# Splitting the mixer's weights during the down projection before it

## The chip, the cores and the metric

The kernel runs on one core of a Trainium2 chip. The metric is the device time of one execution in microseconds; lower is better. The engines are PE (TensorE, matrix products), DVE (VectorE), ACT (ScalarE), POOL (GpSimd) and SP (SyncE, which here only issues DMAs). Each works through its own instructions in order.

## The reference

A first block (attention and a mixture of experts, not touched here) is followed by a second block of two layers on x, 512 tokens of 1024 features, all in float32. Each layer is a gated feed-forward, a mixer and another gated feed-forward, with a layernorm behind each:

```python
def _swiglu(x, wg, wu, wd):
    return (jax.nn.silu(x @ wg) * (x @ wu)) @ wd

def _mixer(x, w_in, ...):
    u = x @ w_in                                        # 1024 -> 1792
    u_conv, u_lru, q, k, v = jnp.split(u, [o1, o2, o3, o4], axis=-1)
    y_conv = _conv_module(u_conv, ...)                  # 31 taps, layernorm, silu
    y_lru = _recurrent(u_lru, ...)                      # 4 taps, gates, linear scan
    y_attn = _swa(q, k, v, band_bias, valid, sinks)     # 8 heads, a band of 128 keys
    return jnp.concatenate([y_conv, y_lru, y_attn], axis=-1) @ w_out

def second_block(x, ...):
    for l in range(DEPTH_2):                            # 2 layers
        h = 0.5 * _swiglu(x, ffn_w_gate[l, 0], ffn_w_up[l, 0], ffn_w_down[l, 0])
        x = _layernorm_2(ALPHA * x + h, ln_g[l, 0], ln_b[l, 0])
        h = _mixer(x, w_in[l], ...)
        x = _layernorm_2(ALPHA * x + h, ln_g[l, 1], ln_b[l, 1])
        h = 0.5 * _swiglu(x, ffn_w_gate[l, 1], ffn_w_up[l, 1], ffn_w_down[l, 1])
        x = _layernorm_2(ALPHA * x + h, ln_g[l, 2], ln_b[l, 2])
    return x
```

## The kernel before

Activations lie feature-major, [128 features, 8 blocks, 512 tokens]. Every float32 product is made of three faster ones (`mm3`, lines 191 to 197): weights and operands are split into a high part (a rounded copy, `wh`, `xh`) and the rest (`wl`, `xl`), and PE adds low times high, high times low and high times high. Activations are split where they are made. Weights are split on the way from DRAM, each time they are used: `chunk` (lines 153 to 167) loads 2048 columns, 1 MB, through SP's queue into one of two buffers `raw`, and `split` (lines 185 to 187) casts each piece of up to 1024 columns on ACT to `wh` and subtracts on DVE to `wl`. The pool `spl` has four buffers for `wh` and four for `wl`, so that a piece can be split when PE has done with the piece four before it. The loads and the splits of a chunk are given a priority ahead of the work around them (`AHEAD`); a scheduler turns priorities and dependences into one fixed order for each engine.

`second` (lines 1447 to 1454) runs six phases: feed-forward 0, mixer 0, feed-forward 1, feed-forward 2, mixer 1, feed-forward 3. A feed-forward (`ffn`, lines 1124 to 1151) makes 22 gated tiles `hh`, `hl` and then the down projection, a loop over d = 0 to 7: 66 products into `y` with pieces of 1024, 1024 and 768 columns of `w_d`, and for each d the layernorm's sums (`Norm.sums`: `x<-x,y` on DVE, line 1047, a square `q` on ACT, line 1054). The last d goes by halves of the tokens, so that `Norm.finish` (statistics, then the norm's outputs `xh`, `xl`) can work on the first half while PE does the second. `Norm.finish` also starts the next phase's first two weight chunks (`first_chunks`). The next phase begins with `first_tiles` (products `ft`), by halves too. The operand lies in the pool `xs`, four buffers [128, 2048]: two for `xh`, two for `xl`; they are in use until the last gate or up product, and again when the next norm writes its outputs.

The mixer (lines 1184 to 1444): the first four tiles; `project(j)` (lines 1228 to 1235) for the chunks 2, 6, 4 and, between the attention steps, 5 and 3 of `w_in2`, two output tiles `t` each; then eight attention steps. `scores` makes the scores in PSUM, DVE adds the bias and takes the maximum (line 1304), ACT the exponential `p` (line 227), DVE scales; `values` transposes `p` on PE (`pT`), copies it on ACT to `pt` (line 1338) and multiplies with the values on PE (`po`, line 1342). The scores of two steps are ahead of the values. On DVE the 62 taps of the convolution (`acc`, line 1220) fill the time from the first tiles on. The out projection takes the four chunks of `w_out2`: 0 from the seventh attention step on, 1 and 2 behind the attention (2 in buffers of its own, `qh` and `ql`), 3 at the end, with the mixer's layernorm by halves.

POOL does two memsets and two small loads (`bt`, the bias, and `wg`) at the start of a mixer, and nothing in a feed-forward.

Of the kernel before, what the change touches and what calls it, by code (L numbers as in the profile page):

```python
# [7 lines left out]
F32 = mybir.dt.float32  # L8
F32R = mybir.dt.float32r
# [5 lines left out]
P = 128  # L15
# [13 lines left out]
PIECE = 1024  # L29
# [33 lines left out]
class Pieces:  # L63
    """2048 columns of weights in DRAM, taken 512 at a time in small buffers"""
# [10 lines left out]
class Core:  # L75
    """The engines, the pools and the pieces that every phase uses."""
# [34 lines left out]
    @contextmanager  # L111
    def banks(self, **tags):
        """the 8 banks of PSUM for a phase: how many for a tag; a name that is no tag counts as any"""
        with self.tc.tile_pool(name="psum", bufs=1, space=bass.MemoryType.PSUM, reuse_waits="tile") as pool:
            old, self.psum = self.psum, (pool, tags)
            yield
            self.psum = old
# [27 lines left out]
    def more_raws(self, *sources, own_first=False):  # L145
        """buffers for loads before the two of every phase: (pool, tag, how many)"""
        self.raws, self.turn, self.pair = [], -1, None
        for pool, tag, n in sources + ((self.rawp, "raw", 2),):
            self.raws = self.raws + [(pool, tag)] * n
        if own_first:  # L150
            self.turn -= 2

    def chunk(self, src, n=2048, room=None):
        """n columns of weights in two parts each: pieces of up to 1024 columns"""
        with self.tc.high_priority(offset=self.ahead):
            r = self.load(src, n) if src.space == bass.MemoryType.DRAM else src
            w = Weights()
            for o in range(0, n, PIECE):
                m = min(PIECE, n - o)
                if room is None:  # L160
                    h = self.spl.tile([P, PIECE], F32R, name="wh", tag="wh")
                    l = self.spl.tile([P, PIECE], F32R, name="wl", tag="wl")
                else:
                    h, l = room(o)
                self.split(h[:, :m], l[:, :m], r[:, o:o + m])
                w.append((h, l))
        return w

    def first_chunks(self, src, early):
        """the two first chunks of a phase, loaded ahead, and four steps that split them; some are done ahead too"""  # L170
# [28 lines left out]
    def rstd(self, out, ssq, n, eps):  # L199
        """out = 1 / sqrt(ssq / n + eps): a first value from the tables, then a step of Newton's"""  # L200
# [14 lines left out]
    def table(self, func):  # L215
        """the table of func is at hand: the tables' loads and their uses keep their order"""
# [7 lines left out]
    def act(self, out, x, func, **more):  # L224
        """an activation that needs a table"""
        self.table(func)
        i = self.nc.scalar.activation(out, x, func, **more)
        self.queue(i, self.loaded)
        self.users.append(i)
# [8 lines left out]
    def new_xs(self, name):  # L238
        """a [feature, 8, 512] operand in two parts: tiles for k = 0..3 and 4..7"""
# [7 lines left out]
def ada_rows(c, cst, j):  # L247
    """column chunk j of the conditioning: rows c hi, c lo, ctx hi, ctx lo and, from chunk 4 on, bias"""
# [16 lines left out]
def ada_store(c, cst, j, dst):  # L265
    """chunk j for c, into the row dst of DRAM"""
# [9 lines left out]
def rms_in(c, x, n):  # L276
    """x [128, 8, n] over the rms of its features, in place"""
# [12 lines left out]
def modulate(c, x, n, cols, cond, hi, lo):  # L290
    """(1 + scale) and shift of x [128, 8, n], split"""
# [9 lines left out]
def head_norm(c, ps, ms, n, gain):  # L301
    """per-head rms (two heads of 64 on the partitions, squares summed in ms) and gain; returns [128, n]"""
# [7 lines left out]
def first_attention(c, x, cst, v_dram, ada_dram):  # L310
    """x holds the tokens feature-major; returns yh, yl (merged, feature-major)"""
    nc, tc, a = c.nc, c.tc, c.a
    with ExitStack() as st:
# [46 lines left out]
        def heads(w, xh, xl, n, gain, done):  # L360
            """two tiles of heads; the norm of the tiles before comes after the products of these"""
# [225 lines left out]
def moe_route(c, lg, R, between):  # L587
    """expert slots from the router's logits lg [128 tokens, 4 tiles, 4 groups + 16 experts]

    The expert of the first overflow block changes places with the last one, unless it is among the FIXED first, and the  # L590
    block shares its weights. Returns the slots' rows and weights of the blocks in their places (a spare row of its own
    for an empty slot) for the FIXED first, for all of them with that block, and for the other overflow blocks; and the
    experts of the latter, their number, and the experts of all the places."""
# [6 lines left out]
    def top(v, g, name):  # L600
        """the largest of every four of v [128, 4 tiles, g, 4] and the one-hot of the first that equals it"""
# [29 lines left out]
    def chosen(v, name):  # L631
        """v [128, 4, 16] or [128, 1, 16] at the experts of the two choices [128, 8]"""
# [110 lines left out]
class Expert:  # L743
    """one block of up to 128 tokens through one expert, in steps that the caller interleaves"""
# [7 lines left out]
    def weights(self, n):  # L752
        """the sources are chunks ready for use, loaded chunks or chunks in DRAM"""
# [16 lines left out]
    def up(self, w, *twin):  # L770
        """a twin is another block with the same weights"""
# [23 lines left out]
    def down(self, *twin):  # L795
        """the output, scaled; with a twin each of the two's in two parts"""
# [25 lines left out]
def first_rest(c, yh, yl, ada_dram, hf_dram, x_dram):  # L822
    """out projection, residual and the experts; returns the tokens feature-major"""
    nc, tc, a = c.nc, c.tc, c.a
    with ExitStack() as st:
# [26 lines left out]
        def scaled(i, nh):  # L852
            """half nh of the features of token tile i of x: the squares' sum, and the part of the experts' input without
            its factor for the token"""
# [6 lines left out]
        def norm(i):  # L861
            """the factors of token tile i of x"""
# [13 lines left out]
        def router(g, nh, h):  # L876
            """half nh of the products of rows h with the router's weights"""
# [155 lines left out]
class Norm:  # L1033
    """layernorm over the features of r = ALPHA * x + y, feature-major, in place of x, by halves of the tokens"""
# [57 lines left out]
def token_stats(c, s, q, n, mu, rs, pS, pQ):  # L1092
    """mean and 1 / deviation of every token on all the partitions, from sums of n features"""
# [9 lines left out]
def first_tiles(c, w, xh, xl):  # L1103
    """the first four output tiles after a norm, by halves of the tokens, as the features come"""
# [9 lines left out]
def tiles2(c, w, xh, xl):  # L1114
    """two output tiles [128, 512] of a chunk of weights"""
# [8 lines left out]
def ffn(c, x, xh, xl, w, i, nxt):  # L1124
    nc, tc, a = c.nc, c.tc, c.a
    with tc.tile_pool(name="ffn", bufs=1, reuse_waits="tile") as R:
# [15 lines left out]
        for d in range(KD):  # L1142
            y = c.ps("y")
# [10 lines left out]
def softplus_cols(c):  # L1154
    """4 * softplus(-lam) of all the channels [128, 4]"""
# [28 lines left out]
def mixer(c, x, xh, xl, w, i, nxt):  # L1184
    nc, tc, a = c.nc, c.tc, c.a
    v2 = c.v2
    with ExitStack() as st:
# [40 lines left out]
        def project(j):  # L1228
            """the two output tiles of chunk j, one at a time"""
            w = c.chunk(a["w_in2"][i, j])  # L1230
# [139 lines left out]
        for j in range(8):  # L1370
# [4 lines left out]
            if j == 6:  # L1375
                w.append(c.chunk(a["w_out2"][i, 0]))
# [6 lines left out]
        w.append(c.chunk(a["w_out2"][i, 1]))  # L1383
        yo[2:] = [c.ps("yo") for _ in range(2)]
        first_out((6, 7), range(2))
        w3 = c.chunk(a["w_out2"][i, 2], room=lambda o: tuple(v[:, o:o + PIECE] for v in wq))
# [50 lines left out]
        w.append(c.chunk(a["w_out2"][i, 3]))  # L1437
# [9 lines left out]
def second(c, x, xh, xl, w):  # L1447
    gu, wi = c.a["w_gu"], c.a["w_in2"]
    phases = [(ffn, 0, gu[0]), (mixer, 0, wi[0]), (ffn, 1, gu[1]), (ffn, 2, gu[2]), (mixer, 1, wi[1]), (ffn, 3, gu[3])]
    with c.banks(any=6,yo0=2):  # L1450
        for j, (phase, i, _) in enumerate(phases):
            norm = phase(c, x, xh, xl, w, i, phases[j + 1][2] if j < 5 else None)
# [11 lines left out]
def host(i):  # L1464
    """the inputs laid out for the chip"""
# [123 lines left out]
```

## Time and profile before

| | |
|---|---|
| runs of the kernel (us) | 2601.84, 2604.46, 2605.72; median 2604.46 |
| profiled execution, span from its first to its last instruction (us) | 2609.7 |
| mean granted clock of PE over the span | 0.973 |
| busy: PE, DVE, ACT, POOL | 96%, 56%, 42%, 3% |
| moved by DMA | 347.98 MB, mean 133 GB/s |
| of it read from and written to DRAM | 329.67 MB and 16.27 MB |

For the profiled execution the profile gives the span alone; it is the time against which durations of the trace are added up, and it stands 5.2 us above the median of the three runs. Times of the trace are microseconds from the span's start. The first mixer with its down projection lies at 1028 to about 1350, the second at 1933 to about 2255.

### The profile page before, as it was taken

What the parts mean: (1) busy time and instruction counts of PE and PEld (TensorE: products, weight loads), DVE (VectorE), ACT (ScalarE), POOL (GpSimd) and SP (SyncE); (2) the same over time, 40 slices, a digit from 0 to 9 for tenths busy, and PEclk for the clock granted to TensorE, in tenths of its full rate; (3) what the DMA queues carried; (4) which work ended last, traced back from release to release, by engine and by line L of the source; (5) the groups of instructions that cost most, each with busy time, mean ns of one, the idle gap of its engine ahead of it and who ended that gap; (6) DMA issues with size and microseconds to landing.
All of it is one profiled execution on the core that took longest, in us unless ns stands there. A gap on an engine that the chain in (4) does not pass through costs nothing.

```text
span 2609.7 us, 31098 instructions
## 1 busy us (share of the span) xinstructions
PE 2506.2 (96%) x12305; PEld 2053.6 (79%) x12305; DVE 1470.2 (56%) x2441; ACT 1106.2 (42%) x1681; POOL 85.9 (3%) x103
## 2 busy tenths in 40 slices
PE   7998987999999999999999999999999999999997
PEld 5786556788878888887688888888888877888886
DVE  6736656899973333369973333453333698633334
ACT  6524532788852222244652232342222546522222
POOL 0010110112100000000000000000000000000000
PEclk8997978999999999999999999999999999999998
DMA  6242456899952222232122222222223311222231
GB/s 258 81 125 93 158 183 238 328 389 393 394 187 72 97 97 93 89 108 86 58 85 97 97 92 90 100 90 97 97 85 107 120 65 65 81 97 97 77 105 61
DMA packets 59524, 347.98 MB, mean 133 GB/s; under 512 B 8832, under 2 KB 11040, under 8 KB 23280
## 3 DMA queue, kind: packets, MB, share of 16 engines
q1 hardware_dynamic: 47776, 311.45, 32.5%
q0 software_dynamic: 10448, 31.86, 4.2%
q10 hardware_dynamic: 1152, 2.66, 0.3%
q8 instruction: 97, 1.59, 0.3%
q14 instruction: 51, 0.42, 0.0%
HBM read 329.67 MB, written 16.27 MB: 133 GB/s over the span
## 4 chain that ended last, share of the span: by engine, by line
PE 69%; DVE 8%; ACT 3%; issue 1%; DMA 0%; DVEq 0%; ACTq 0%; another core or an unknown queue 0%; SPq 0%
PE t L195 12%; PE t L196 12%; PE t L197 12%; PE y L195 7%; PE y L197 7%; PE y L196 7%; PE e L195 2%; PE e L197 2%; PE e L196 2%; DVE acc L1220 2%; DVE wl L187 1%; PE ft L195 1%; PE ft L196 1%; PE ft L197 1%; ACT x L1083 1%
## 5 line engine op out<-in xcount | busy, mean ns | idle before, releaser
L186 ACT CAST wh<-raw 128x1024 fp32r<-128x1024 f32 x552 | 571.0, 1039 | 1107.7 <-PE t L197 353.2
L187 DVE TENSOR_TENSOR wl<-raw,wh 128x1024 fp32r<-128x1024 f32 x552 | 658.4, 1207 | 653.4 <-ACT wh L186 649.3
L195 PE MATMUL t<-xh,wl 128*128 128x512 f32 x1440 | 561.5, 390 | 0.0
L196 PE MATMUL t<-xl,wh 128*128 128x512 f32 x1440 | 560.5, 389 | 0.0
L197 PE MATMUL t<-xh,wh 128*128 128x512 f32 x1440 | 560.3, 389 | 0.0
L195 PEld LDWEIGHTS t<-xh,wl 128*128 128x128 f32 x1440 | 270.3, 188 | 58.4 <-issue 2.3
L196 PEld LDWEIGHTS t<-xl,wh 128*128 128x128 f32 x1440 | 270.4, 188 | 56.3 <-issue 0.8
L197 PEld LDWEIGHTS t<-xh,wh 128*128 128x128 f32 x1440 | 270.3, 188 | 56.2
L195 PE MATMUL y<-hh,wl 128*128 128x512 f32 (+1 forms) x792 | 289.8, 366 | 2.1 <-DVE x L1047 2.1
L196 PE MATMUL y<-hl,wh 128*128 128x512 f32 (+1 forms) x792 | 290.1, 366 | 0.0
L197 PE MATMUL y<-hh,wh 128*128 128x512 f32 (+1 forms) x792 | 289.4, 365 | 0.0
L1133 DVE SCALAR_TENSOR_TENSOR s<-s,t 128x512 f32<-128x512 f32 x80 | 55.1, 688 | 254.4 <-PE t L197 254.4
L195 PEld LDWEIGHTS y<-hh,wl 128*128 128x128 f32 x792 | 149.3, 189 | 26.9 <-DVE x L1047 2.9
L196 PEld LDWEIGHTS y<-hl,wh 128*128 128x128 f32 x792 | 149.4, 189 | 24.2
L197 PEld LDWEIGHTS y<-hh,wh 128*128 128x128 f32 x792 | 149.4, 189 | 24.2
L195 PE MATMUL ft<-xh,wl 128*128 128x256 f32 x384 | 104.1, 289 | 8.3 <-ACT xh L1088 7.0
L196 PE MATMUL ft<-xl,wh 128*128 128x256 f32 x384 | 109.8, 290 | 0.7 <-DVE xl L1089 0.7
L195 PE MATMUL e<-wh,hTl 128*128 128x512 f32 x272 | 108.7, 399 | 0.5 <-issue 0.5
L197 PE MATMUL ft<-xh,wh 128*128 128x256 f32 x384 | 108.1, 286 | 0.0
L197 PE MATMUL e<-wh,hTh 128*128 128x512 f32 x272 | 106.9, 393 | 0.0
L196 PE MATMUL e<-wl,hTh 128*128 128x512 f32 x272 | 106.8, 393 | 0.0
L1220 DVE SCALAR_TENSOR_TENSOR acc<-yp,hw,acc 128x512 f32<-128x512 f32 x120 | 85.2, 745 | 0.1
(475 smaller groups left out, 3565.8 us busy)
## 6 DMA issues: line engine op xcount, KB each, us to landing
raw<-in_w_gu SPq DMA_DIRECT2D x88, 1024.0 KB, 4.7
raw<-in_w SPq DMA_DIRECT2D x82, 1024.0 KB, 12.0
raw<-in_w_d SPq DMA_DIRECT2D x32, 1024.0 KB, 4.9
raw<-in_w_ada SPq DMA_DIRECT2D x24, 1024.0 KB, 4.8
pair<-in_w SPq DMA_DIRECT2D x14, 1024.0 KB, 12.9
raw<-in_w_in SPq DMA_DIRECT2D x14, 1024.0 KB, 4.7
raw<-in_w_out SPq DMA_DIRECT2D x12, 1024.0 KB, 4.7
raw<-in_w_d SPq DMA_DIRECT2D x32, 384.0 KB, 3.1
```

What stands on the lines that cost most here:

```text
L186: self.nc.scalar.copy(h, x)
L187: self.nc.vector.tensor_sub(l, x, h.bitcast(F32))
L195: mm(ps, al, bh, start=first, stop=False)
L196: mm(ps, ah, bl, start=False, stop=False)
L197: mm(ps, ah, bh, start=False, stop=last)
L1083: nc.scalar.activation(r, t, AF.Identity, bias=b[:, d:d + 1], scale=g[:, d:d + 1])
L1133: nc.vector.scalar_tensor_tensor(s, s, 0.5, ps[1], op0=OP.mult, op1=OP.mult)
L1220: nc.vector.scalar_tensor_tensor(acc[:, t], yp[:, t, j:j + S], w, acc[:, t], op0=OP.mult, op1=OP.add)
```

## The change

Nine of the eleven chunks of weights of a mixer (w_in2 chunks 2, 6, 4, 5, 3 and w_out2 chunks 0 to 3) are no longer split in the mixer. `parted` loads such a chunk through POOL's queue, splits it (a cast and a subtraction of 2048 columns), and stores the two parts, 1 MB each, into a tile in DRAM. It works in three buffers of the pool `xs`, in turn over its four. The down projection of feed-forward 0 does this for mixer 0, that of feed-forward 2 for mixer 1: one, two, one, two, one, two chunks ahead of the products of d = 0 to 5. In the mixer, `ready_chunk` loads the low and the high part of each piece, 512 KB each, through SP's queue straight into the buffers `wl` and `wh` (or `ql` and `qh`). The first two chunks of w_in2 and all other weights are split as before.

```diff
+    def parted(self, src, dst):
+        r, h, l = (self.xs.tile([P, 4, 512], F32, name=n, tag="xs").rearrange("p a n -> p (a n)") for n in ("pr", "ph", "pl"))
+        self.nc.gpsimd.dma_start(r, src)
+        self.split(h.bitcast(F32R), l.bitcast(F32R), r)
+        self.nc.gpsimd.dma_start(dst[0], h)
+        self.nc.gpsimd.dma_start(dst[1], l)
+
+    def ready_chunk(self, src, room=None):
+        with self.tc.high_priority(offset=self.ahead):
+            w = Weights()
+            for o in range(0, 2048, PIECE):
+                if room is None:
+                    h = self.spl.tile([P, PIECE], F32R, name="wh", tag="wh")
+                    l = self.spl.tile([P, PIECE], F32R, name="wl", tag="wl")
+                else:
+                    h, l = room(o)
+                for part, t in ((1, l), (0, h)):
+                    self.nc.sync.dma_start(t.bitcast(F32), src[part, :, o:o + PIECE])
+                w.append((h, l))
+        return w
...
-def ffn(c, x, xh, xl, w, i, nxt):
+def ffn(c, x, xh, xl, w, i, nxt, more):
...
         for d in range(KD):
+            for m in more[d * 3 // 2:(d + 1) * 3 // 2]:
+                c.parted(*m)
             y = c.ps("y")
...
-def mixer(c, x, xh, xl, w, i, nxt):
+def mixer(c, x, xh, xl, w, i, nxt, parts):
...
-            w = c.chunk(a["w_in2"][i, j])
+            w = c.ready_chunk(parts["in", j])
...
-                w.append(c.chunk(a["w_out2"][i, 0]))
+                w.append(c.ready_chunk(parts["out", 0]))
...
-        w.append(c.chunk(a["w_out2"][i, 1]))
+        w.append(c.ready_chunk(parts["out", 1]))
...
-        w3 = c.chunk(a["w_out2"][i, 2], room=lambda o: tuple(v[:, o:o + PIECE] for v in wq))
+        w3 = c.ready_chunk(parts["out", 2], room=lambda o: tuple(v[:, o:o + PIECE] for v in wq))
...
-        w.append(c.chunk(a["w_out2"][i, 3]))
+        w.append(c.ready_chunk(parts["out", 3]))
...
     phases = [(ffn, 0, gu[0]), (mixer, 0, wi[0]), (ffn, 1, gu[1]), (ffn, 2, gu[2]), (mixer, 1, wi[1]), (ffn, 3, gu[3])]
+    order = [("in", j) for j in (2, 6, 4, 5, 3)] + [("out", j) for j in range(4)]
...
-            norm = phase(c, x, xh, xl, w, i, phases[j + 1][2] if j < 5 else None)
+            if phase is mixer:
+                more = parts
+            else:
+                more = []
+                if j < 5 and phases[j + 1][0] is mixer:
+                    n = phases[j + 1][1]
+                    parts = {key: c.dram.tile([2, P, 2048], F32, name="%s%d_%d" % (key + (n,))) for key in order}
+                    more = [(c.a["w_in2" if key[0] == "in" else "w_out2"][n, key[1]], parts[key]) for key in order]
+            norm = phase(c, x, xh, xl, w, i, phases[j + 1][2] if j < 5 else None, more)
```

The rest of the difference is docstrings that are left out, which shifts the line numbers by some twenty.

Two engines' orders show how the instructions move. ACT at the end of the first down projection, before the change (`wh` are the pieces of `w_d`, `q` the squares of the layernorm, the last of them for the first half of d = 7, `mu` its mean):

```order
434 L186 CAST wh<-raw 128x1024
435 L1054 ACTIVATE q<-x_6604 128x512
436 L186 CAST wh<-raw 128x1024
437 L186 CAST wh<-raw 128x768
438 L186 CAST wh<-raw 128x1024
439 L1054 ACTIVATE q<-x_6604 128x512
440 L186 CAST wh<-raw 128x1024
441 L186 CAST wh<-raw 128x768
442 L186 CAST wh<-raw 128x1024
443 L1054 ACTIVATE q<-x_6604 128x512
444 L1054 ACTIVATE q<-x_6604 128x256
445 L1097 ACTIVATE mu<-pS 128x256
```

and now, with `ph`, the cast of a part:

```order
442 L209 CAST wh<-raw 128x1024
443 L209 CAST ph<-pr 128x2048
444 L209 CAST wh<-raw 128x768
445 L209 CAST wh<-raw 128x1024
446 L1077 ACTIVATE q<-x_6604 128x512
447 L209 CAST wh<-raw 128x1024
448 L209 CAST ph<-pr 128x2048
449 L209 CAST wh<-raw 128x768
450 L209 CAST wh<-raw 128x1024
451 L1077 ACTIVATE q<-x_6604 128x512
452 L209 CAST ph<-pr 128x2048
453 L1077 ACTIVATE q<-x_6604 128x256
454 L1120 ACTIVATE mu<-pS 128x256
```

Nine casts of 2048 columns stand among the others in this loop, the last of them between the square of d = 6 and that of the first half of d = 7. DVE's order has the subtraction `pl` in the corresponding places, the last one right ahead of the add `x<-x,y` of that half.

DVE in the first mixer, from the split of the keys (`kl`) to where the queries are split (`ql`), before (`wl` are pieces of weights, `acc` the taps):

```order
892 L187 TENSOR_TENSOR wl<-raw,wh 128x1024
893 L187 TENSOR_TENSOR kl<-t_9543,kh 128x512
894 L1220 SCALAR_TENSOR_TENSOR acc<-yp,hw,acc 128x512 x6
895 L187 TENSOR_TENSOR wl<-raw,wh 128x1024
896 L1220 SCALAR_TENSOR_TENSOR acc<-yp,hw,acc 128x512 x9
897 L1280 SCALAR_TENSOR_TENSOR ql<-t_9615,qh 128x512
898 L187 TENSOR_TENSOR wl<-raw,wh 128x1024
899 L1220 SCALAR_TENSOR_TENSOR acc<-yp,hw,acc 128x512 x5
900 L1280 SCALAR_TENSOR_TENSOR ql<-t_9642,qh 128x512
901 L1220 SCALAR_TENSOR_TENSOR acc<-yp,hw,acc 128x512
902 L187 TENSOR_TENSOR wl<-raw,wh 128x1024
903 L1220 SCALAR_TENSOR_TENSOR acc<-yp,hw,acc 128x512 x5
```

and now:

```order
896 L1246 SCALAR_TENSOR_TENSOR acc<-yp,hw,acc 128x512 x2
897 L210 TENSOR_TENSOR kl<-t_9620,kh 128x512
898 L1246 SCALAR_TENSOR_TENSOR acc<-yp,hw,acc 128x512 x17
899 L1306 SCALAR_TENSOR_TENSOR ql<-t_9690,qh 128x512
900 L1246 SCALAR_TENSOR_TENSOR acc<-yp,hw,acc 128x512 x7
901 L1306 SCALAR_TENSOR_TENSOR ql<-t_9717,qh 128x512
902 L1246 SCALAR_TENSOR_TENSOR acc<-yp,hw,acc 128x512 x7
903 L1330 ISA sc,sm<-sc,bt 128x128
```

The subtractions `wl` are gone, taps stand in their places, and the first bias and maximum (an ISA row) follow behind them.

POOL in the down projection, where before there was nothing, repeats this pattern of a load and two stores nine times:

```order
99 L172 DMA pr<-in_w_in 128x2048
100 L174 DMA in_0_6752<-ph 128x2048
101 L175 DMA in_0_6752<-pl 128x2048
102 L172 DMA pr<-in_w_in 128x2048
103 L174 DMA in_0_6753<-ph 128x2048
104 L175 DMA in_0_6753<-pl 128x2048
```

The next part's load stands behind the stores of the one before on the same queue.

## Rows read from the trace of the kernel before

**Rows 1.** The page: the span, and each engine's busy us, share and instructions.

```profile
span 2609.7 us, 31098 instructions
...
PE 2506.2 (96%) x12305; PEld 2053.6 (79%) x12305; DVE 1470.2 (56%) x2441; ACT 1106.2 (42%) x1681; POOL 85.9 (3%) x103
```

**Rows 2.** Windows: length, busy PE PEld DVE ACT POOL, PE clock, DMA share, GB/s.

```profile
1028.00:1140.00 112.00, 112.00 (x525) 93.99 (x524) 38.82 (x44) 25.85 (x30) 0.00 (x0) 1.00 0.29 97
...
1176.00:1275.00 99.00, 90.89 (x479) 66.20 (x477) 97.20 (x238) 53.51 (x136) 0.00 (x0) 1.00 0.24 85
1275.00:1320.00 45.00, 44.40 (x284) 39.82 (x284) 39.81 (x74) 24.00 (x37) 0.00 (x0) 1.00 0.14 48
```

**Rows 3.** Waits of PE, 1176 to 1350: us in total, times, longest.

```profile
PE po L1342 <- ACT pt L1338: 5.5, 6, 1.8
PE ft L195 <- ACT xh L1088: 2.1, 2, 1.9
PE vT L1273 <- ACT v L1270: 1.6, 1, 1.6
```

**Rows 4.** Chain that ended last, 1196 to 1226: start, us, what.

```profile
1200.15 1.14 DVE wl L187
...
1218.01 0.21 DVE sc L1304
...
1223.92 0.93 ACT wh L186
1224.85 0.28 ACT pt L1338
```

**Rows 5.** DVE's groups, 1176 to 1297: count, busy us, mean ns, idle before.

```profile
L1220 DVE SCALAR_TENSOR_TENSOR acc<-yp,hw,acc 128x512 f32<-128x512 f32 x60 | 42.7, 751 | 0.1
L187 DVE TENSOR_TENSOR wl<-raw,wh 128x1024 fp32r<-128x1024 f32 x11 | 13.5, 1223 | 0.2 <-ACT wh L186 0.2
```

**Rows 6.** Timeline of ACT, then of PE: start, us, instruction, idle before and its releaser.

```profile
1198.26 1.04 ACT L186 CAST wh<-raw 128x1024 fp32r<-128x1024 f32 x1 [3.90 <-PE t L197]
1199.22 0.58 ACT L1270 COPY v<-t 128x512 f32<-128x512 f32 x1
...
1261.01 2.05 ACT L186 CAST qh<-raw 128x1024 fp32r<-128x1024 f32 x2
...
1263.97 1.57 PE L1342 MATMUL po<-pt,vt 128*64 128x256 f32 x8 [1.31 <-ACT pt L1338]
```

**Rows 7.** Groups of ACT and DVE in the down projection, 1028 to 1140.

```profile
L186 ACT CAST wh<-raw 128x1024 fp32r<-128x1024 f32 x15 | 15.8, 1051 | 52.6 <-PE y L197 49.8 <-PE t L197 2.8
L186 ACT CAST wh<-raw 128x768 fp32r<-128x768 f32 x7 | 5.9, 837 | 30.7 <-PE y L197 30.7
...
L187 DVE TENSOR_TENSOR wl<-raw,wh 128x1024 fp32r<-128x1024 f32 x15 | 18.3, 1223 | 25.3 <-ACT wh L186 25.3
```

**Rows 8.** Timeline of PE where the down projection begins, and where the mixer begins.

```profile
1027.94 0.39 PE L195 MATMUL y<-hh,wl 128*128 128x512 f32 x1
...
1150.25 0.62 PE L195 MATMUL ft<-xh,wl 128*128 128x256 f32 x3
```

**Rows 9.** Timeline of POOL at the mixer's start.

```profile
1145.90 0.60 POOL L1197 DMA_DIRECT2D bt<-in_rel  x1 [1.58 <-PE y L197]
```

**Rows 10.** Windows of 1 us behind that issue; the last number is GB/s.

```profile
1147.00:1148.00 1.00, 1.00 (x11) 1.00 (x10) 1.00 (x2) 0.00 (x0) 0.10 (x1) 1.00 0.84 131
1148.00:1149.00 1.00, 1.00 (x10) 1.00 (x10) 0.96 (x3) 0.85 (x1) 0.00 (x0) 1.00 0.93 393
...
1152.00:1153.00 1.00, 1.00 (x10) 0.95 (x9) 1.00 (x4) 1.00 (x2) 0.00 (x0) 1.00 1.04 442
```

**Rows 11.** DMA issues: queue, count, KB each, median us from issue to landing.

```profile
raw<-in_w_gu SPq DMA_DIRECT2D x88, 1024.0 KB, 4.7
...
bt<-in_rel POOLq DMA_DIRECT2D x1, 1024.0 KB, 5.0
```

**Rows 12.** Timeline of DVE at the add of the last tile's first half.

```profile
1140.77 0.42 DVE L1047 SCALAR_TENSOR_TENSOR x<-x,y 128x256 f32<-128x256 f32 x1 [4.76 <-PE y L197]
```

## The prediction

> **What bounds the kernel now.** First the busy shares of the page: PE is busy 2506.2 of 2609.7 us, DVE 56%, ACT 42% [rows 1]. So time is to be had only where PE stands, and lost wherever PE is made to stand. The times of this text are those of this execution; the median of the runs shown, 2604.46 us, is 5.2 lower, and I take that off at the end. Then the windows by stage, for the first of the two mixers, which run the same code [rows 2]: in the down projection before the mixer (1028 to 1140) PE is busy all 112.00 us, with DVE at 38.82 and ACT at 25.85. In the mixer's middle (1176 to 1275) it is the other way: DVE is busy 97.20 of 99 us and PE 90.89, so PE stands 8.1 us there, and 0.6 more up to 1320, 8.7 together. The waits of PE say for what: 5.5 us in six waits of the products with the values (po) for ACT's copies pt, 1.6 for the copy v [rows 3]. The chain of waits through this stretch runs over DVE: taps with weight splits between them (wl, 1.14), until the first bias and maximum at 1218.01; then over ACT, where the copy pt comes behind a weight cast (wh, 0.93) [rows 4]. Of DVE's time from 1176 to 1297, 60 of the 62 taps take 42.7 us, and eleven splits of weights 13.5 [rows 5]; with two more of 1.2 (`ql` from `raw`) 15.9. That is what the change takes out of the mixer.
>
> **What is removed, and what it is worth.** In each mixer 18 casts of 128x1024 on ACT and as many subtractions on DVE go. The order of DVE shows that taps move up into their places and the first softmax instruction stands as far behind the taps as it did. The most that can come back is what PE stood, 8.7 us (2.1 more in the next first tiles [rows 3], of which a little might go too). The least is nothing: if the scores' latency, not the casts, sets the waits, they stay. I price it by the casts in front of the copies. The copy v waits behind a cast of 1.04 that began before it, and a copy pt behind two of together 2.05, begun at 1261.01; PE stood 1.31 us for it, to 1263.97 [rows 6]. The chain shows the same at 1223.92 [rows 4]. So most of the 5.5 for pt and about 1.0 of the 1.6 for v hang on a cast or split ahead in the same queue: **6.5 us per mixer, 13.0 for both**; ends 0 and 8.7 + 1.
>
> **What is added in the down projection.** Nine parts pass through one chain: a load on POOL's queue, a cast of 2048 columns, a subtraction of 2048 columns, a store of the high part, a store of the low part, and behind that on the same queue the next load. No row has 2048 columns; casts take 1051 ns at 1024 and 837 at 768, subtractions 1223 at 1024 [rows 7]. By the slope a cast takes 1.9 us, 0.2 less than two of 1024; likewise a subtraction 2.3 (2.45 at most). On ACT that is 9 x 1.9 = 17 us and on DVE 21 us within a stretch of 112 where they are busy 26 and 39: the work itself is covered, since the w_d pieces are cast as PE frees their buffers: a piece of 1024 columns is 24 products, of which PE does 495 (7.5 x 66) in the 112 us of the window, 0.226 each, so 5.4 us, and three pieces ahead are 16. Less cast and split of 2.3, some 13 us remain, and by the chain below a part's cast holds ACT's queue at most some 5 beyond its place. Cost 0; if the cover were gone, each late piece would cost what it is late.
>
> The chain's length is what counts. A load or store of 1 MB has no row on an otherwise idle queue. From POOL's issue at 1145.90 [rows 9] data flow from about 1147.1, and then 393 to 442 GB/s [rows 10]: 1.2 us to the first byte, 2.5 us for 1 MB. A 1 MB load lands 4.7 to 5.0 us after its issue [rows 11], so about 1.0 remains for the end. After the subtraction the low part's store must be issued (0.15 + 1.2 to its data), moved (2.5), then the next load moved (2.5) and closed (1.0): 7.35. With cast, subtraction and hand-overs of 0.1, 7.35 + 1.9 + 2.3 + 0.1 = 11.65 us per part. In between, 1 MB and 384 KB of w_d come every 15 us, 3.3 us of transfers on the same engines; I add 1.2 for sharing: **12.9 us per part**. The ends: 11.3 (no sharing, the end of a load 0.6), and 14.5 if store and load do not overlap at all and each takes the 5.0 of the row (0.15 + 5.0 + 5.0 + 4.3).
>
> The projection begins at 1027.94 and its first half of the last tile is added at 1140.77 [rows 8, 12], 112.8 later. That add is now queued on DVE behind the last subtraction, and the square on ACT behind the last cast, as the order shows. The first load can't leave before 1027.94, because its buffers hold the operand of the gate and up products. Its cast ends at 5.0 + 1.3 (for the share of w_d) + 1.9 = 8.2; the last subtraction ends at 8.2 + 8 x 12.9 + 2.35 = 113.75. So the add comes 0.95 late. What waits for it is the layernorm of the first half, whose result PE needs at 1150.25 [rows 8], 122.3 after the start; a little later ft waits for xh [rows 3], so I count no slack: late by 1 us there is 1 us. **Cost: 1 per mixer, 2.0 together**, nothing up to 12.7 us per part, and 8 us for each us above. The norm's operand takes the buffers of the last stores, which land about 2.6 and 4.9 after the last subtraction, at 116.4 and 118.6, in time for 122.3.
>
> **What is loaded in the mixer.** Nine loads of 1 MB become 36 of 512 KB on SP, 27 more issues, at the 0.6 us of a POOL issue [rows 9] 16 us on a queue that does little else in 170 us: 0. A piece is now two transfers into the buffer that PE freed, some 4.7 to 5.0 us, where a cast and a split took 2.3. With 5.4 us of PE per piece and three ahead, 16 us, the loads are covered. If that cover were gone, a piece would cost 2.7. I take 0, between 0 and two such pieces per mixer. POOL's 27 DMAs per projection take 0.6 each on an idle engine: 0; its memsets and the bias load bt are now queued behind the last store's issue, but the first score, which needs bt, comes at 1218.01 [rows 4], 72 us after bt's issue.
>
> **Sum:** -13.0 + 2.0 = -11.0: 2598.7 for this execution, **2593.5** for the median.
>
> **The rivals.**
> *The chain of parts is longer (slower).* Place: the add of the first half of the last tile. From 13.6 us per part on, the delay (8 x 13.6 + 10.55 - 112.8 = 6.55) eats the gain; at 14.5 it is 13.75 per mixer, and the time 2604.5 - 13 + 27.5 = 2619. For it: the first two chunks of w_in2 are also loaded in the last 10 us, and no row shows POOL's queue with a load behind a store. Against it: the rate in [rows 10], and that the transfers leave the engines idle two thirds of the stretch (share 0.29 [rows 2]). The rate decides much of it: at 2.9 us per MB instead of 2.5 the part takes 13.7, the delay is 7.35 and the time 2606; I give that a quarter of this rival's chance.
> A rule to this effect stands in the Trainium skill, "DMA: Bandwidth & Descriptors", Specifications: about 358 GB/s as one core's limit to its DRAM, which would be 2.93 us per MB. The windows show 393 to 442 GB/s, so the trace disagrees with it and sides with "HBM Reference", Specifications, by which a core that streams alone reaches some 425.
> *The waits stay.* The softmax's own chain (scores, maximum, exponential, transpose, copy) sets the time of pt, and the casts only filled it. Then 2 us per mixer come back: 2604.5 - 4 + 2 = 2602.5. For it: the taps move up ahead of the scores and keep DVE as full as before. Against it: what stands right ahead of pt is a cast, twice.
> *The parts do not come ready.* The pieces' loads, not their casts, become what the projections of the mixer wait for, first after the first tiles, where the buffers come free late. Two pieces late by 2.7: 2593.5 + 2 x 5.4 = 2604. For it: 5.0 against 2.3 us; against: 16 us ahead.
>
> **How the numbers follow.** Forecast 0.54, longer chain 0.22, waits stay 0.16, parts not ready 0.08. A measurement of this kernel tells some 0.2%, 5.2 us, from no change: below 2599 is faster, above 2610 slower. Faster: 0.54 and a third of the second rival, 0.59. Slower: the first rival without its quarter at 2606, 0.17. The same: the rest, 0.24. The range: below, all 8.7 + 1 per mixer with no delay is 2604.5 - 19.4 = 2585; above, it reaches into the first rival to 14.2 us per part, a delay of 11.35 per mixer: 2604.5 - 13 + 22.7 = 2614. The forecast's own range is 2585 to 2599.
>
> **What would show it.** Right: from 1176 to 1320 DVE 16 us less busy, PE idle some 2 instead of 8.7, the weights' casts gone from the chain; in the projection nine casts of 1.9 us and nine subtractions of 2.3 some 12.9 apart, the last one done within 114 us of the first y product; the add at 112.8 to 114. Wrong: ft waiting longer at 1150 for xh or xl behind a late part (first rival); po waiting for pt by the same 5.5 (second); t2 products waiting for DMA (third). If the time falls by more than 20 us, something besides the casts held PE that I did not see.

## The result and the profile after

The change makes the kernel slower: 2631.89 us (median of four runs, 2628.56 to 2638.82) against 2603.15 before, a ratio of 1.0113 with a 95% interval of 1.0094 to 1.0132. Forecast were 2593.5 us, and 2585 to 2614.

The spans of the two profiled executions do not show this by themselves, since the unchanged first block took 12 us less in the profile of after than in that of before. So I divide the time from the first `ft` and `y` products on PE's timeline, which begin each phase. A projection runs from the first `y` to the next `ft`; "mixer and up" from a mixer's first `ft` over the next phase's gate and up products to its first `y`.

| us | projection 0 | projection 2 | mixer 0 and up | mixer 1 and up |
|---|---|---|---|---|
| before | 122.3 | 122.3 | 416.6 | 416.7 |
| after | 143.7 | 138.0 | 412.0 | 413.6 |

The two projections lose 21.4 and 15.7 us, the two mixers give back 4.5 and 3.1: +29.5, near what the medians show (+28.7). Both the gain and the cost are other than forecast: 3.8 instead of 6.5 per mixer, and 18.6 instead of 1.0.

That the two mixers after differ is not the work of the change. Windows over mixer 0 and up before, mixers 0 and 1 and up after, and a stretch inside the last (columns as in [rows 2]: length, then PE's busy time; behind POOL's, PE's clock):

```profile
1150.25:1566.80 416.55, 404.07 (x2110) 335.74 (x2109) 259.94 (x514) 186.70 (x337) 0.00 (x0) 1.00 0.25 86
1159.57:1571.58 412.01, 402.84 (x2109) 334.19 (x2109) 240.57 (x496) 169.47 (x319) 0.00 (x0) 1.00 0.32 110
2075.55:2489.11 413.56, 404.39 (x2110) 335.08 (x2110) 240.58 (x496) 169.50 (x319) 0.00 (x0) 1.00 0.32 110
2160.60:2163.80 3.20, 3.20 (x10) 2.00 (x7) 1.14 (x6) 2.02 (x9) 0.00 (x0) 0.50 0.00 0
```

PE stands 12.5 us before and 9.2 in both mixers after, so the waits give 3.3 us. The 1.6 us between mixer 0 and mixer 1 after are PE's clock: in mixer 1 the granted clock was 0.50 for a short stretch, the lower of its two levels (1.2 GHz), right behind a wait of 1.9 us; mixer 0 had such a wait too, and no such stretch. Both mixers before have one. So lengths of mixers are compared below where the clock is the same, or by the time that PE stands.

The page of after, to be read beside [rows 1]: the span is longer, PE and DVE are about as busy as before, and the group of `y` products has 32.5 us of idle time in front of it, 27.6 of them behind an add on DVE.

```profile
span 2626.6 us, 31294 instructions
...
PE 2497.8 (95%) x12305; PEld 2047.9 (78%) x12305; DVE 1470.3 (56%) x2423; ACT 1103.4 (42%) x1663; POOL 114.6 (4%) x157
...
L218 PE MATMUL y<-hh,wl 128*128 128x512 f32 (+1 forms) x792 | 292.3, 369 | 32.5 <-DVE x L1070 27.6
```

The waits of PE from 1020 to 1380, the first projection and mixer, beside [rows 3]:

```profile
PE y L218 <- DVE x L1070: 12.4, 1, 12.4
PE y L218 <- DVE wl L210: 4.6, 2, 3.9
PE ft L218 <- ACT xh L1111: 3.0, 3, 1.9
PE po L1368 <- DVE ql L1306: 1.9, 1, 1.9
PE po L1368 <- ACT pt L1364: 1.6, 4, 0.9
...
PE vT L1299 <- ACT v L1296: 0.7, 1, 0.7
```

In the mixer the wait of `po` for `pt` has fallen from 5.5 to 1.6 us and that for `v` from 1.6 to 0.7, but a wait of 1.9 for `ql` is new. In the projection PE waits 17.0 us, where it waited 0.5 before. The chain that ended last shows how they end, from the last part's load to the second half of the last tile (start, us, what):

```profile
1131.27 12.08 DMA pr<-in_w_out
1143.42 1.91 ACT ph L209
1145.35 2.29 DVE pl L210
1147.64 0.34 DVE x L1070
1148.03 0.58 PE y L218
```

This is the place that the first rival named. The projection began at 1015.85 and the last subtraction ended at 1147.6, 131.8 us later, instead of the 113.75 worked out; the add came 18.9 us after its time in [rows 12]. Note the load: 12.08 us for 1 MB from its issue. The parts come at this pace (POOL's timeline, the stores of the second, third and ninth part and two loads: start, us, instruction, idle before):

```profile
1037.83 0.53 POOL L174 DMA_DIRECT2D in<-ph  x1 [11.93 <-ACT ph L209]
1040.15 0.53 POOL L175 DMA_DIRECT2D in<-pl  x1 [1.79 <-DVE pl L210]
1040.70 0.54 POOL L172 DMA_DIRECT2D pr<-in_w_in  x1
1054.18 0.53 POOL L174 DMA_DIRECT2D in<-ph  x1 [12.94 <-ACT ph L209]
1056.51 0.53 POOL L175 DMA_DIRECT2D in<-pl  x1 [1.79 <-DVE pl L210]
1058.10 0.54 POOL L172 DMA_DIRECT2D pr<-in_w_in  x1 [1.05 <-issue]
...
1145.61 0.53 POOL L174 DMA_DIRECT2D out<-ph  x1 [13.80 <-ACT ph L209]
```

From the first store of a high part (1022.32) to the ninth (1145.61) are 123.3 us: 15.4 per part, not 12.9 (14.8 in the second projection). The windows show what fills one (columns as in [rows 2]):

```profile
1024.00:1036.00 12.00, 12.00 (x54) 9.95 (x53) 3.80 (x6) 2.17 (x3) 1.07 (x2) 1.00 0.94 360
1036.00:1038.00 2.00, 2.00 (x10) 1.66 (x9) 1.41 (x2) 2.00 (x3) 0.17 (x1) 1.00 0.00 0
1039.00:1051.00 12.00, 12.00 (x55) 9.94 (x54) 4.33 (x5) 0.84 (x1) 1.07 (x2) 1.00 0.98 374
1051.00:1055.00 4.00, 4.00 (x19) 3.34 (x18) 1.08 (x1) 3.02 (x3) 0.53 (x1) 1.00 0.03 10
```

For 12 us the DMA engines are full (share 0.94 and 0.98), then for 2 to 4 us they stand while ACT casts. In 12 us at 360 to 374 GB/s move some 4.4 MB, which is three transfers of a part (3.1 million bytes) and most of the 1.4 of `w_d` that belong to every `d`. And in these stretches the loads of `w_d` themselves land late, 8.6 us after their issue instead of 4.9 (the median of before; DMA issues from 1016 to 1148):

```profile
raw<-in_w_d SPq DMA_DIRECT2D x6, 1024.0 KB, 8.6
...
pr<-in_w_in POOLq DMA_DIRECT2D x4, 1024.0 KB, 10.2
pr<-in_w_out POOLq DMA_DIRECT2D x4, 1024.0 KB, 10.4
```

My theory after this: the loss is the chain of nine parts at 15.4 us against a deadline, the add of the last tile's first half; the mixer itself gains a little. The rivals: a cost for each part wherever it runs, or something on the reading side.

### The profile page after: what moved, and what is told of

The parts are those of the page before. It is cut to its first block, busy times and chain, and to the rows that moved or that the text cites. A ratio compares the mean times of both kernels' runs of the same rounds, so it can differ in the third digit from the quotient of the medians.

```text
span 2626.6 us, 31294 instructions
## 1 busy us (share of the span) xinstructions
PE 2497.8 (95%) x12305; PEld 2047.9 (78%) x12305; DVE 1470.3 (56%) x2423; ACT 1103.4 (42%) x1663; POOL 114.6 (4%) x157
## 4 chain that ended last, share of the span: by engine, by line
PE 38%; issue 36%; DVE 4%; DMA 3%; ACT 2%; POOL 1%; DVEq 0%; ACTq 0%; POOLq 0%; another core or an unknown queue 0%; SPq 0%
PE t L219 6%; PE t L218 6%; PE t L220 6%; PE y L218 3%; PE y L220 3%; PE y L219 3%; PE e L218 2%; PE e L220 2%; PE e L219 2%; DMA pr<-in_w_out 1%; DMA raw<-in_w_d 1%; PE ft L218 1%; PE ft L219 1%; PE ft L220 1%; PE gT L788 1%
## 5 line engine op out<-in xcount | busy, mean ns | idle before, releaser
L210 DVE TENSOR_TENSOR wl<-raw,wh 128x1024 fp32r<-128x1024 f32 (+1 forms) x520 | 619.1, 1207 | 559.7 <-ACT wh L209 555.8
L209 ACT CAST wh<-raw 128x1024 fp32r<-128x1024 f32 (+1 forms) x520 | 536.3, 1038 | 933.0 <-PE t L220 317.7
L218 PE MATMUL y<-hh,wl 128*128 128x512 f32 (+1 forms) x792 | 292.3, 369 | 32.5 <-DVE x L1070 27.6
L210 DVE TENSOR_TENSOR pl<-pr,ph 128x2048 fp32r<-128x2048 f32 x18 | 41.3, 2293 | 116.4 <-ACT ph L209 116.4
## 6 DMA issues: line engine op xcount, KB each, us to landing
raw<-in_w SPq DMA_DIRECT2D x82, 1024.0 KB, 11.7
pair<-in_w SPq DMA_DIRECT2D x14, 1024.0 KB, 12.5
```

Source lines behind the costliest of these rows:

```text
L209: self.nc.scalar.copy(h, x)
L210: self.nc.vector.tensor_sub(l, x, h.bitcast(F32))
L218: mm(ps, al, bh, start=first, stop=False)
```

## The experiments

**One part only, the mixer as in the change.** All nine chunks of the mixer are read from one prepared tile, so its weights are not the right ones; eight parts are left out.

```diff
-                    parts = {key: c.dram.tile([2, P, 2048], F32, name="%s%d_%d" % (key + (n,))) for key in order}
-                    more = [(c.a["w_in2" if key[0] == "in" else "w_out2"][n, key[1]], parts[key]) for key in order]
+                    one = c.dram.tile([2, P, 2048], F32, name="one%d" % n)
+                    parts = {key: one for key in order}
+                    more = [(c.a["w_in2"][n, 2], one)]
```

> One part is prepared per mixer instead of nine, and all nine chunks of the mixer are read from its two halves in DRAM, so that the mixer is that of the change (the weights are not the right ones) while the down projection is nearly that of before. Theory (the cost lies in the chain of nine parts, 15.4 us each, and the mixer itself gains only some 2.7 us): both mixers about 167 and 168.5 us from first ft to first ft, the projections 122 to 123, ratio to before 0.997 to 0.999 (about 2597). Rival (the mixer gains the 6.5 us forecast, but starts disturbed by what the late parts leave behind): mixers 163 to 165 us, ratio about 0.995 or less.

Ratio 0.9962 (0.9946 to 0.9978). Both projections took 122.3 us, mixer and up 413.7 and 412.2, as in the change (412.0 and 413.6), again one with the stretch of the lower clock and one without. So the mixer of the change gains 3.7 us, whether parts were late before it or not; the forecast of 6.5 was too high.

**The parts alone.** They are prepared and never read; the mixer calls `chunk` as before.

> The nine parts are prepared and stored in the projection as in the change, but the mixer splits its weights itself as before and never reads them. Theory: the projections stay at 138 to 144 us as in the change, the mixers are those of before (about 170), ratio about 1.014 (2603 + 37 = 2640). Rival (part of the loss comes from the reading side, the loads of the parts in the mixer): projections shorter than 135, ratio 1.008 or less.

Ratio 1.0151 (1.0134 to 1.0168); projections 144.1 and 138.4, mixer and up 417.8 and 417.0. The whole loss lies in preparing. The two experiments add up to the change: -0.38% and +1.51% make +1.13%.

**Five parts, of w_in2 alone.**

> Only the five chunks of w_in2 are prepared; the four of w_out2 are split in the mixer as before. Theory (chain against a deadline): 6.2 + 4 x 15.4 + 4.2 = 72 us after the first y product the last part is split, 40 us ahead of the add at 112.8, so no delay: projections 122 to 123, mixers 167 to 169, ratio 0.998 to 1.000. Rival (contention: each part costs PE about 2 us whenever it runs, because w_d comes late): five ninths of the loss remain, projections 131 to 134, ratio about 1.006.

Ratio 0.9993 (0.9980 to 1.0006). The projections are back at 122.3 and 122.8: five parts, each as slow as before (casts of the first and fifth at 1030.00 and 1092.66, so 15.7 for each), cost PE nothing. That speaks for a deadline and against a cost per part. But mixer and up stay at 417.3 and 416.2 where I expected some 2 us less, and PE waits for `pt` 5.6 us as ever. Taking away the splits of w_in2 is worth little: PE stands 11.7 and 12.1 us instead of 12.5 and 12.6, about what the wait for `v` fell, and in the first mixer a second stretch of the lower clock hides it.

**Four parts, of w_out2 alone.**

> Only the four chunks of w_out2 are prepared; the five of w_in2 are split in the mixer as before. Theory (the casts of w_out2 are those ahead of the copies pt; five parts of w_in2 alone gave nothing): the last part is split 6.2 + 3 x 15.4 + 4.2 = 57 us after the first y product, no delay; the mixers with the first tiles behind them gain 2 to 3.5 us each, ratio 0.9970 to 0.9985 (about 2598). Rival (a gain only where both kinds of splits are gone): the mixers stay at 170 to 171, ratio 0.999 to 1.000.

Ratio 0.9974 (0.9961 to 0.9987), projections 122.3, mixer and up 412.9 and 412.7: in sum as much as the change gains. The waits of PE in this run:

```profile
PE po L1368 <- DVE ql L1306: 1.7, 1, 1.7
PE vT L1299 <- ACT v L1296: 1.6, 1, 1.6
PE po L1368 <- ACT pt L1364: 1.6, 4, 0.9
```

The wait for `v` is back at 1.6, behind a cast of w_in2. It costs its time: PE stands 10.0 us in each mixer instead of 9.2, and where the clock stays up the stretch takes 412.7 to 412.9 against 412.0 with all nine. That the sum is the same as in the change is luck, for neither has the stretch of the lower clock here. The wait for `pt` has gone from 5.5 to 1.6 and takes most of the time with it. It was the casts and splits of w_out2, run ahead into the attention, that stood in front of the copies.

**The load of a part from ACT's queue.** It no longer stands behind the subtraction and two stores.

```diff
-        self.nc.gpsimd.dma_start(r, src)
+        self.nc.scalar.dma_start(r, src)
```

> The load of a part is issued from ACT's queue, right behind the cast of the part before, instead of from POOL's behind both stores; all else is the change. Theory (the next load stands behind the subtraction and two stores): it starts some 4 us earlier and runs beside the subtraction and the stores; a part then takes what its transfers need, 4.4 MB at about 400 GB/s, 11 to 12 us, the last subtraction ends at 6.2 + 8 x 11.5 + 2.3 = 100 us, and nothing is late: projections 122 to 124, ratio about 0.998. Rival (transfers and the casts of w_d lock each other: the parts' casts wait in ACT's order behind those of w_d, whichever queue loads them): a part still takes 14 to 15 us, projections 133 to 144, ratio 1.007 or more.

Both were half right. A part takes 11.2 us on the mean (casts of the first and ninth at 1023.22 and 1112.46, 89.2 for eight; by turns 5 and some 17 us apart), so the place of the load in the queue was worth 4 us; and the add is on time, 0.5 us of wait. Yet the ratio is 1.0133 (1.0116 to 1.0150) and the projections take 141.0 and 141.2. PE now waits for something else, the splits of `w_d`, for a reason that the run with seven parts on this queue will show (waits, 1020 to 1162; and a window of the stretch with the parts):

```profile
PE y L218 <- DVE wl L210: 14.4, 4, 6.3
PE y L218 <- DVE x L1070: 0.5, 1, 0.5
```

```profile
1023.00:1115.00 92.00, 80.49 (x344) 65.20 (x342) 39.21 (x33) 31.05 (x26) 8.98 (x17) 0.96 0.87 337
```

**Without the stores of the low parts.** The kernel leaves them out, and the mixer loads the high part in their place.

```diff
-        self.nc.gpsimd.dma_start(dst[1], l)
...
-                for part, t in ((1, l), (0, h)):
+                for part, t in ((0, l), (0, h)):
```

> The change without the stores of the low parts (the mixer loads the high part twice, so its weights are not the right ones). Theory (a cycle is some 3.4 us without transfers and all its transfers in series with them at 360 to 375 GB/s): 3.5 MB instead of 4.6 make 9.3 us, the part 12.7 or less, the last subtraction ends at 6.2 + 8 x 12.7 + 2.3 = 110 us, the add is on time, projections 122 to 126. Rival (fixed times of queue and casts make the cycle): a part takes over 14 us and the projections stay over 130.

A part takes 10.4 us (casts at 1019.56 and 1102.44, eight of them apart), the last is split 92 us after the first `y` product, both projections take 122.3 us, and the one run took 2592.13 us with all nine chunks read in parts. The store carries 5.0 us of the 15.4: its own transfer of 1 MB, and, as the load then no longer waits for the subtraction on POOL's queue, that wait too; I had counted the first alone.

**Seven and eight parts.** With `order` without w_in2 2 and 6, and without 2 alone.

```diff
-    order = [("in", j) for j in (2, 6, 4, 5, 3)] + [("out", j) for j in range(4)]
+    order = [("in", j) for j in (4, 5, 3)] + [("out", j) for j in range(4)]
...
-            w = c.ready_chunk(parts["in", j])
+            w = c.ready_chunk(parts["in", j]) if ("in", j) in parts else c.chunk(a["w_in2"][i, j])
```

> Seven chunks are prepared: w_in2 4, 5, 3 and w_out2 0 to 3; w_in2 2 and 6, used before the attention, are split as before. Theory (chain against a deadline): the last part is split 6.2 + 6 x 15.4 + 4.2 = 102.8 us after the first y product, before the add at 112.8: projections 122 to 123, mixers near those with one part alone (168.6 and 167.1), ratio 0.996 to 0.998. Rival (w_d is held up as soon as parts run most of the time): projections 126 to 132, ratio 1.001 or more.

> Eight chunks are prepared (as the seven, and w_in2 6). Theory: the last part is split 6.2 + 7 x 15.4 + 4.2 = 118.2 us after the first y product, 5.4 past the add at 112.8: projections 126 to 129, between the 122 of seven parts and the 138 to 144 of nine. Rival (no deadline, a cost per part): 133 to 138.

Seven parts: ratio 0.9971 (0.9960 to 0.9982), 2595.68 us, projections 122.3 both, mixer and up 412.1 and 413.6. The last part's subtraction on DVE ends at 1112.2, 98.6 us after the first `y` product at 1013.57, and the add comes in its time (DVE's timeline):

```profile
1109.89 2.29 DVE L210 TENSOR_TENSOR pl<-pr,ph 128x2048 fp32r<-128x2048 f32 x1 [8.86 <-ACT ph L209]
...
1126.40 0.42 DVE L1070 SCALAR_TENSOR_TENSOR x<-x,y 128x256 f32<-128x256 f32 x1 [0.56 <-PE y L220]
```

Eight parts: projections 128.9 and 123.7, between seven and nine. The first lies in the range expected, the second under it, and not for the reason given: the last part was done 113.3 us after the first `y` product, hardly late for the add. PE waited instead for a piece of `w_d` whose cast and subtraction stand behind that part's in the orders of ACT and DVE:

```profile
PE y L218 <- DVE wl L210: 3.5, 1, 3.5
PE y L218 <- DVE x L1070: 0.5, 1, 0.5
```

So there are two deadlines close together: the last pieces of `w_d`, and the add. Most of the rest of the 6.6 us that the first projection loses is PE's clock, 0.50 for a stretch behind that wait.

**Seven parts with the load on ACT's queue.**

> Seven parts, but their loads issued from ACT's queue as in e5, which made a part take 11.2 instead of 15.4 us. Theory (a shorter chain makes the transfers collide: with the parts at 11.2 us each the DMA engines are full, the pieces of w_d come late, and ACT, which works in order, holds both up): PE waits 8 to 12 us for splits of w_d in the first projection, which takes 130 to 134 us; slower than the seven parts on POOL's queue (122.3), though the parts are done earlier. Rival (only the deadline of the last part counts): projections 122 to 124.

Ratio 1.0087 (1.0053 to 1.0120), projections 135.0 both, a microsecond more than expected. The seven parts are done earlier than on POOL's queue (last cast 71 us after the first `y` product against 94), and 12.7 us per projection are lost:

```profile
PE y L218 <- DVE wl L210: 10.4, 3, 6.6
```

```profile
1024.00:1094.00 70.00, 62.89 (x275) 51.03 (x273) 28.53 (x25) 23.42 (x20) 6.50 (x12) 1.00 0.86 332
```

A shorter chain is worse here. With the loads on POOL's queue the engines' mean share is 0.76 while seven parts run, and PE does not stand at all:

```profile
1016.00:1112.00 96.00, 96.00 (x425) 79.47 (x425) 42.52 (x39) 32.61 (x30) 10.14 (x19) 1.00 0.76 289
```

My theory had the engines full, the pieces of `w_d` therefore late, and ACT, in order, holding up both. ACT's timeline ahead of the longest of the three waits, which ends at 1097.30, shows the last part of this alone:

```profile
1082.56 1.05 ACT L209 CAST wh<-raw 128x1024 fp32r<-128x1024 f32 x1 [6.89 <-DMA out<-pl]
...
1091.88 1.90 ACT L209 CAST ph<-pr 128x2048 fp32r<-128x2048 f32 x1 [7.75 <-DMA pr<-in_w_out]
1093.69 1.77 ACT L209 CAST wh<-raw 128x1024 fp32r<-128x1024 f32 x2
```

The piece that PE waits for was there: the first half of its 1 MB had been cast at 1082.56. Its own cast stands behind that of the last part, for whose load ACT waited 7.75 us. The cast at 1082.56 in turn stood behind the issue of that load, which waited on ACT for a store to free its buffer. With the loads on POOL's queue the order is another: there the seventh part's cast stands ahead of the last piece of `w_d` for d = 6, here ahead of the second for d = 4. So in this wait, the longest, PE pays for ACT's fixed order, in which the parts were moved ahead of `w_d`, and not for a load of `w_d`. A chain as short, in the run without the low parts' stores (10.4 us per part), lost nothing, though it had one store less to move.

**The new wait for ql.** The seven parts, with the subtraction `ql` of the query tiles 2 and 3 at a higher priority.

```diff
             nc.scalar.mul(qh[m], ps, 0.125)
-            nc.vector.scalar_tensor_tensor(ql[m], ps, 0.125, qh[m].bitcast(F32), op0=OP.mult, op1=OP.subtract)
+            with tc.high_priority(offset=40 if m > 1 else 0):
+                nc.vector.scalar_tensor_tensor(ql[m], ps, 0.125, qh[m].bitcast(F32), op0=OP.mult, op1=OP.subtract)
```

> The seven-part version with one priority changed: DVE's subtraction ql of the query tiles 2 and 3 goes ahead of taps and of three of the four scalings p, 0.85 us earlier for tile 3. Theory (the one wait of 1.9 us that is left before po is for a bank of PSUM that ql still reads, because DVE does taps and scalings first): that wait falls to about 1.0 us and each mixer is 0.5 to 0.9 us shorter than 167.0 and 168.5. Rival (po waits for the copy pt in any case): the wait turns into one for pt, mixers the same within 0.3 us.

The wait fell more than expected, with a small one in another place:

```profile
PE t L218 <- DVE ql L1307: 0.6, 1, 0.6
...
PE po L1369 <- DVE ql L1307: 0.4, 1, 0.4
```

Mixer and up took 411.4 and 412.8, against 412.1 and 413.6 with the seven parts alone, and in both runs it is the second that has the stretch of the lower clock; PE stands 8.6 us instead of 9.4 in each. So some 0.75 us per mixer have gone with the wait, as expected, in one execution of each kernel. The single run took 2598.32 us, within what the seven parts alone took (2589.03 to 2598.94), so the time of the whole kernel does not show it.

## Why the prediction was wrong

**What bounds the kernel** was read rightly in the main: time came back and was lost where PE stood, and beside that by PE's clock, which I had not counted. **The first rival was the truth**: a longer chain that ends at that add, beyond its far end; what made it longer it named only in part. I gave it 0.22.

**The step that failed** is this: "In between, 1 MB and 384 KB of w_d come every 15 us, 3.3 us of transfers on the same engines; I add 1.2 for sharing: **12.9 us per part**." From the low part's store to the landing of the next load that is 8.55 us with the sharing; measured are 11.1, what is left of 15.4 when cast, subtraction and hand-overs (4.3, as forecast) are taken off. I let two transfers of a part and a third of `w_d`'s lie in the chain. In the trace nearly everything lies in it, some 4.4 MB in 12 us with the engines 0.94 to 0.98 busy, then nothing for about 3 us. By the orders it is no accident that they collide: the casts of `w_d` stand behind the casts of parts in ACT's order, so the buffers of `w_d` come free, and its loads start, together with the stores of the part (in the second cycle at 1041.02, the part's own next load at 1040.70). That `w_d` does it is read from the trace; no run took its transfers out, while the run without the low parts' stores shows what one store weighs. The rate was a small part of it: I took 2.5 us per MB, some 420 GB/s, from single microseconds of [rows 10], and 12 us of loads and stores together ran at 360 to 374. My far end of 14.5 left `w_d` out altogether. And a mean share of 0.29 in [rows 2] was no argument against a collision: it is the share over a stretch, and the chain is what decides when the transfers come.

The multiplication behind it held: eight parts at 2.5 us more each are 20 us, and the add was 18.9 late against the 0.95 forecast. The 2 us between come from the start: I had said that the first load can't leave before the first `y` product, and it left 2.5 us ahead of it (1013.37), so that the first cast ended at 6.2 and not at 8.2. What that does to PE was named too mildly: not only the layernorm of the first half waits, but the `y` products of the second half wait for the add itself (12.44 us). In the trace of before that wait is there too, 0.5 us long, and I had passed over it.

**The gain** had the right mechanism and the wrong size. "So most of the 5.5 for pt and about 1.0 of the 1.6 for v hang on a cast or split ahead in the same queue: 6.5 us per mixer": the waits did fall by 3.9 and 0.9, but 1.9 came back as the wait for `ql`, which reads a bank of PSUM that `po` needs and stands on DVE behind taps and scalings. Measured were 3.8, to the end of the next up products; 3.4 of it are time that PE no longer stands, the rest is the clock of mixer 0. In the mixer's middle, where I wanted PE to stand some 2 us instead of 8.7, it stood 6.1. Four parts of w_out2 gave most of this, five of w_in2 the 0.5 to 0.8 of the wait for `v`. The second rival, that the waits stay, was thus about half true in its number, but not in its reason: the wait for `pt` did hang on the casts.

**What was priced at nothing** mostly was nothing: the 36 loads in the mixer (no wait of PE for a DMA there), POOL's issues (0.53 us each), the middle of the projection until the last tile (110.77 of the first 112 us busy). The third rival did not show: no wait of the projections `t` for a DMA. Cast and subtraction of 2048 columns took 1.91 and 2.29 us, against 1.9 and 2.3 worked out. One was not: that "a part's cast holds ACT's queue at most some 5 beyond its place". ACT stood 6.7 and 10.8 us ahead of the last two parts' casts, with pieces of `w_d` behind the first of them, and PE waited 4.6 us for `w_d` in the first projection (0.2 in the second).

A rule of the Trainium skill that I set aside, about 358 GB/s for a core ("DMA: Bandwidth & Descriptors", Specifications), lies nearer to these stretches, at 360 to 374, than the 420 I took. But the trace of before does not bear it out as a limit, in a stretch of the first block in which full DMA engines mostly load:

```profile
520.00:740.00 220.00, 219.56 (x1046) 183.29 (x1045) 212.94 (x220) 176.16 (x196) 40.44 (x24) 1.00 1.01 385
```

There 385 GB/s were moved over 220 us, and at shares of 0.94 and 0.98 that is the rate of the stretches with stores as well. So neither the rule's limit nor the mixing of loads and stores is needed to explain them: the 420 was that of single microseconds. At 385 a MB takes 2.7 us, an estimate by which the rate makes up some 0.5 of the 2.5 us that a part was longer.

## What to carry to other kernels

Work that is moved into a stage with idle engines must be priced as a chain, with every transfer of that stage in it, and its end set against the first instruction that stands behind it in a queue: here nine parts cost 37 us and seven cost nothing. Move only what stands in front of something: four of the nine chunks carried most of the gain, and the version with them, or with seven, is 0.3% faster than the kernel before. And a chain that is made shorter can lose, if its instructions are thereby put ahead of another stream's in the fixed order of an engine that both use.

## What the runs showed that I had not expected

PE's clock added to the loss. In the first projection PE stood 3.92 us, up to 1131.38, for a piece of `w_d`; in that wait the granted clock fell to 0.50, the lower of its two levels (1.2 GHz), and it was 0.76 on the mean of the stretch after the 12.44 us of standing:

```profile
1131.00:1135.60 4.60, 4.21 (x18) 3.91 (x18) 3.35 (x5) 0.63 (x1) 0.81 (x2) 0.50 1.02 342
1135.60:1148.00 12.40, 0.00 (x0) 0.00 (x0) 2.62 (x2) 1.90 (x1) 0.60 (x2) 0.50 0.59 249
1148.00:1159.60 11.60, 11.57 (x71) 11.03 (x71) 7.56 (x17) 4.91 (x9) 1.80 (x5) 0.76 0.56 222
```

The last products of `y` came every 0.21 us where they had come every 0.12, and the second half with its statistics took 11.5 us instead of 9.0. Of the 21.4 us that this projection lost, 16.5 are waits (17.0 against 0.5), and most of the other 4.9 is this: such a wait costs more than it lasts.
